# Seven block products instead of eight in the second feed-forward product of a decoder block, its operand sums kept in DRAM

## The chip, the cores and the metric

The kernel runs on one core of one Trainium2 chip. The metric is the time of one execution in microseconds (us), as the median of several runs. A profile comes from one further execution, so its time is given beside its span. The engines are PE (TensorE), DVE (VectorE), ACT (ScalarE), POOL (GpSimd) and SP (SyncE, which here issues all DMAs from one queue, in order); PEld is the loading of PE's stationary operand.

## The reference

A decoder block over 1024 tokens of width 1024, in float32: a state-space branch and a forgetting-attention branch, merged by gates, then cross-attention into 256 memory tokens, then a SwiGLU feed-forward part and a final RMS norm. What matters here is the end:

```python
f_a, f_b = jnp.split(rms_norm(h, norm_ffn[l]) @ w_ffn_in[l], 2, axis=-1)
h = h + (jax.nn.silu(f_a) * f_b) @ w_ffn_out[l]
return rms_norm(h, norm_final)
```

`w_ffn_in` is 1024 x 5632, `w_ffn_out` is 2816 x 1024. So there are 22 tiles of 128 hidden channels, or 11 pairs.

## The kernel before

Every product of float32 operands is made of three matmuls of rounded parts. `split` (L172 to L174) makes the parts: ACT casts a tile to its high part (L173), DVE subtracts that from the tile to get the low part (L174); the matmuls are high x high, high x low and low x high.

**First feed-forward product**, for each hidden tile j of 22 (`start`, `middle`, `end`, L766 and around). It is already done by seven block products in place of eight, each of 12 matmuls of 128 x 128 by 512, which makes 84 per j. The moving operands A11, A12, S4, A22, S1, S2, S3 are sums of quarters of the normed activations. They are built once: `norm_blocks` stores parts to DRAM and `norm_rest` (L714) reads them back (`xr`) and splits them into S4 and A22. The stationary operands are made for every j from two raw weight tiles of 512 KB, `raw` and `rawb`: `w_fetch` loads them (L723), `w_first` splits the first, `w_sums` forms five sums on DVE (L742 to L749) and splits those, `w_last` splits the rest (`wdh`, `wdl`) and so frees the raw tiles. `raw` has two buffers, so the one for j + 2 is loaded when `w_last` of j is done. `end` makes the gated result g of tile j, 128 channels by 1024 tokens: a DVE operation gives the first half of the tokens (L794), and a DVE add (L796), an ACT activation (L797) and a POOL product (L798) the second. g is stored to DRAM as two tiles of 256 KB (`g_d`, L800). The loop runs `start(j)`, `end(j - 1)`, `w_last(j)`, `middle(j)`, `w_first(j + 1)`, `w_sums(j + 1)`, `w_fetch(j + 2)`.

**Second feed-forward product.** For each half hf of the tokens and each j of 22, `o_get` loads 512 KB of `w_ffn_out` (`raw`) and the 256 KB of g (`gr`), splits both (`woh`/`wol`, `gp`), and `o_mm` adds 24 matmuls into eight PSUM banks: four token tiles by two halves of 512 outputs. Loads run three steps ahead in the text. The last four steps of a half are done token tile by token tile. After each tile DVE adds the bank to the residual `hf` (L895, residual read back from `h_d`), ACT sums the squares (L896), `rsqrt` (L188 to L198, one operation of it on POOL, L192) gives the norm's factor, and `scale` (L865) multiplies and stores the result (L867).

**What sets the order.** The text gives an order, but a scheduler of the language fixes the order on each engine when the kernel is built, by its own estimates, and it can move an instruction far from where the text has it. Each engine then runs its list in order and waits where a semaphore says so; SP does the same with the DMAs. Buffers also order the work: `t` has 16 tiles of 128 x 1024 (12 of them hold A11, A12 and S2 during the first product), `big` 16 (S1, S3, S4 and A22), `tmp` four (`rawb`, g), `half` five, `whi` and `wlo` four each, `gbc` and `xs` one each. In the build of before the load of the final norm's gain into `gbc` (L203) stands right behind the last use of the previous gain, in front of the first product's loop.

The functions that the diff touches, with the lines of the profile:

Of the kernel before, what the change touches and what calls it, by code (L numbers as in the profile page):

```python
# [19 lines left out]
P = 128  # L20
D = 1024
L = 1024
NT = 8
# [7 lines left out]
SLOT = 1040  # L31
# [34 lines left out]
def f32(ap):  # L66
    return ap.bitcast(F32)
# [37 lines left out]
class Shared:  # L105
# [5 lines left out]
    def tmp(self, name, dt=F32):  # L111
        return self.pool.tile([P, D], dt, tag="tmp", bufs=4, name=name)
# [356 lines left out]
def stage_tail(B, big, s2, sh, x, glu, aT, gate_d, kv_d, w_fox_o, w_mix_out, g_mq, w_mem_q, w_mem_o, g_ffn,  # L469
               w_ffn_in, w_ffn_out, g_fin, out):  # L470
    nc, V, A, G, T, S, small, ident = B.nc, B.V, B.A, B.G, B.T, B.S, B.small, B.ident
    NS2 = 16

    def bslot(dt=F32, name="b"):
        return big.tile([P, D], dt, tag="big", name=name)

    def slot(dt=F32, name="t"):
        return s2.tile([P, D], dt, tag="t", bufs=NS2, name=name)

    tmp = sh.tmp  # L480
# [99 lines left out]
    sc = float(DH * 2) ** -0.5  # L580
# [84 lines left out]
    g_d = B.dram.tile([NF, 2, P, 512], F32, name="g_d")  # L665
    comb = {}

    def blocks(name, mk):
# [51 lines left out]
    def w_fetch(j):  # L720
        raws[j] = B.wpool.tile([P, SLOT], F32, tag="raw", bufs=2, name="raw")[:, :D], tmp("rawb")
        for r_, c in zip(raws[j], (0, FH)):
            S.dma_start(r_.rearrange("p (k c) -> p k c", k=8),  # L723
                        w_ffn_in[:, c + j * P:c + (j + 1) * P].rearrange("(k p) c -> p k c", p=P))
# [64 lines left out]

    def end(j):  # L790
        b1, b3, a0, a1, c1 = [ev.pop((j, s_)) for s_ in ("b1", "b3", "a0", "a1", "c1")]
        g = tmp("g")
        prod(j, 3, b1, False)
        V.scalar_tensor_tensor(out=g[:, :512], in0=b1, scalar=-1.0, in1=a0, op0=ALU.mult, op1=ALU.mult)  # L794
        prod(j, 4, b3, False)
        V.tensor_add(a1, a1, b3)  # L796
        A.activation(a1, a1, AF.Silu)  # L797
        G.tensor_mul(g[:, 512:], a1, c1)  # L798
        for h in range(2):
            S.dma_start(g_d[j, h], g[:, 512 * h:512 * h + 512])  # L800
# [37 lines left out]
    gfin = B.bcast_gain(s2, g_fin)  # L838
    LAST = 4
    seq = [(hf, j) for hf in range(2) for j in range(NF)]  # L840
    ops, ssq, rs, Hf = {}, {}, {}, {}

    def o_get(n):
        hf, j = seq[n]
        wr = B.wpool.tile([P, SLOT], F32, tag="raw", bufs=2, name="raw")[:, :D]
        S.dma_start(wr, w_ffn_out[j * P:(j + 1) * P, :])
        gr = sh.half("gr")
        S.dma_start(gr, g_d[j, hf])
        w_ = wpair(0) if n < 3 else (bslot(F32R, "woh"), bslot(F32R, "wol"))
        g_ = slot(F32R, "gp")  # L850
        B.split(*w_, wr)
        B.split(g_[:, :512], g_[:, 512:], gr)
        ops[n] = w_, g_

    def o_mm(n, ps, i, c):
        j = seq[n][1]
        (wh, wl), g_ = ops[n]
        cs = slice(512 * c, 512 * c + 512)
        B.mm3(ps, g_[:, i * P:(i + 1) * P], g_[:, 512 + i * P:512 + (i + 1) * P], wh[:, cs], wl[:, cs],
              j == 0, j == NF - 1)  # L860

    def scale(t):
        for c in range(2):
            cs = slice(512 * c, 512 * c + 512)
            V.scalar_tensor_tensor(out=Hf[t][:, cs], in0=Hf[t][:, cs], scalar=rs[t], in1=gfin[:, cs], op0=ALU.mult,  # L865
                                   op1=ALU.mult)
            S.dma_start(out[t * P:(t + 1) * P, cs], Hf[t][:, cs])  # L867

    for n in range(3):
        o_get(n)  # L870
    end(NF - 1)
    for hf in range(2):
        bk = [B.bank(t_) for t_ in ("mm", "mm", "mm", "sc", "sc", "pv", "pv", "misc")]
        for j in range(NF - LAST):
            n = hf * NF + j
            for i in range(4):
                for c in range(2):
                    o_mm(n, bk[2 * i + c], i, c)
            if n + 3 < len(seq):
                o_get(n + 3)  # L880
            if j == NF - LAST - 4:
                for i in range(4):
                    t = 4 * hf + i
                    Hf[t] = slot(name="hf")
                    S.dma_start(Hf[t], h_d[t])
        n0 = hf * NF + NF - LAST
        o_get(n0 + 3)
        for i in range(4):
            t = 4 * hf + i
            ssq[t] = small.tile([P, 2], F32, name="ssq")  # L890
            for c in range(2):
                cs = slice(512 * c, 512 * c + 512)
                for n in range(n0, n0 + LAST):
                    o_mm(n, bk[2 * i + c], i, c)
                V.tensor_add(Hf[t][:, cs], Hf[t][:, cs], bk[2 * i + c])  # L895
                A.activation(B.junk[:, :512], Hf[t][:, cs], AF.Square, scale=1.0 / 32, accum_out=ssq[t][:, c:c + 1])  # L896
            rs[t] = B.rsqrt(ssq[t], parts=2)
            scale(t)
            if hf == 0 and i < 3:
                o_get(NF + i)  # L900


class Glu:
# [349 lines left out]
class Fox:  # L1253
# [350 lines left out]
```

## Time and profile before

| | us |
|---|---|
| median of 3 runs (1645.52 to 1646.85) | 1646.68 |
| the profiled execution | 1651.04 |
| its span on the core | 1649.2 |
| PE busy | 1580.4 |
| DVE busy | 934.6 |
| ACT busy | 639.2 |
| POOL busy | 256.7 |
| granted clock of PE, mean | 0.976 |

The profile gives for each engine the time in which it was busy; for stretches of the span the same by engine, with the granted clock and what the DMAs moved; for groups of like instructions the busy time, the mean of one in ns, the idle time of the engine just before them and what ended it (`<-`); and single instructions in order of time, with start, duration, line, what is written and what is read. A matmul's duration reaches over the start of the next, so a row of busy time does not say how closely they follow each other. `SPq` and `PEq` are the queues of those engines: an `SPq` row is the issue of a DMA, not its transfer.

### The profile page before, as it was taken

The numbers are of one execution on the slowest core, as the hardware profiler recorded it, in microseconds if no ns is written. First come the engines' busy times: TensorE is split into PE (matmuls) and PEld (weight loads), VectorE is DVE, ScalarE is ACT, GpSimd is POOL, SyncE is SP. The second block draws the span as 40 slices with busy tenths as digits, with TensorE's granted clock in tenths as the row PEclk, the third lists the DMA queues.
The fourth block names the chain that finished last, engine by engine and source line by source line (L and its number), as shares of the span: only waits on it lengthen the run. The fifth ranks groups of instructions, "written<-read, shape, count | busy, mean of one in ns | idle before, by whom it ended". The sixth has DMA issues, their size and how long they took to land. (4 is left out here: it accounts for less than half of the span.)

```text
span 1649.2 us, 20384 instructions
## 1 busy us (share of the span) xinstructions
PE 1580.4 (96%) x7445; PEld 1298.6 (79%) x7445; DVE 934.6 (57%) x1761; ACT 639.2 (39%) x1180; POOL 256.7 (16%) x339
## 2 busy tenths in 40 slices
PE   7899599998999999999999989999999999999998
PEld 6688588897677778888888768888888887888886
DVE  6646564424777777773445798555554554535423
ACT  5322233322566654221325665333333333424311
POOL 2007455100111214210002210000010000000000
PEclk7899799999899999999999999999999999999999
DMA  7655557633312544443211254322223224843721
GB/s 250 132 88 99 59 120 125 148 72 40 41 52 60 141 130 130 139 141 117 81 64 52 94 202 144 97 77 78 83 77 96 87 67 143 297 153 134 243 64 51
DMA packets 202339, 184.26 MB, mean 112 GB/s; under 512 B 48232, under 2 KB 156872, under 8 KB 202240
## 3 DMA queue, kind: packets, MB, share of 16 engines
q1 hardware_dynamic: 202240, 182.97, 41.1%
q8 instruction: 58, 0.95, 0.3%
q14 instruction: 41, 0.34, 0.1%
HBM read 136.76 MB, written 44.14 MB: 110 GB/s over the span
## 5 line engine op out<-in xcount | busy, mean ns | idle before, releaser
L174 DVE TENSOR_TENSOR wlo<-raw,whi 128x1024 fp32r<-128x1024 f32 (+2 forms) x129 | 137.1, 1064 | 217.8 <-ACT whi L173 206.1
L173 ACT CAST whi<-raw 128x1024 fp32r<-128x1024 f32 (+2 forms) x132 | 119.2, 906 | 264.5 <-DMA raw<-in_w_in_dram 75.2
L163 PE MATMUL mm<-uh,whi 128*128 128x512 f32 x344 | 140.4, 408 | 0.3 <-DVE mc L1423 0.3
L165 PE MATMUL mm<-uh,wlo 128*128 128x512 f32 x344 | 138.2, 402 | 0.0
L164 PE MATMUL mm<-ul,whi 128*128 128x512 f32 x344 | 137.9, 401 | 0.0
L174 DVE TENSOR_TENSOR wol<-raw,woh 128x1024 fp32r<-128x1024 f32 x41 | 50.2, 1225 | 105.7 <-ACT woh L173 105.4
L798 POOL TENSOR_TENSOR g<-a,c 128x512 f32<-128x512 f32 x22 | 33.8, 1537 | 394.1 <-ACT a L797 394.1
L173 ACT CAST woh<-raw 128x1024 fp32r<-128x1024 f32 x41 | 43.0, 1049 | 112.5 <-PE misc L164 92.8
L192 POOL TENSOR_TENSOR r<-ms,mhalf 128x1 f32<-128x1 f32 x26 | 17.4, 670 | 387.3 <-DVE ms L188 379.1
L165 PEld LDWEIGHTS mm<-uh,wlo 128*128 128x128 f32 x344 | 66.7, 194 | 13.7 <-DVE wlo L174 0.2
L163 PEld LDWEIGHTS mm<-uh,whi 128*128 128x128 f32 x344 | 67.2, 195 | 13.0 <-DVE mc L1423 0.6
L164 PEld LDWEIGHTS mm<-ul,whi 128*128 128x128 f32 x344 | 66.7, 194 | 11.8
L1455 POOL TENSOR_TENSOR pl<-pf,ph 128x512 fp32r<-128x512 f32 (+1 forms) x32 | 36.9, 1152 | 237.9 <-DVE ph L1454 223.3
L1452 ACT ACTIVATE pf<-sc 128x512 f32<-128x512 f32 (+1 forms) x96 | 46.4, 490 | 49.9 <-DVE sc L1448 34.0
L766 PE MATMUL pv<-S3h,we 128*128 128x512 f32 x176 | 58.8, 394 | 2.0 <-ACT S3h L173 2.0
L163 PE MATMUL mm<-woh,gp 128*128 128x512 f32 x123 | 47.8, 389 | 0.0
L164 PE MATMUL mm<-wol,gp 128*128 128x512 f32 x123 | 47.8, 389 | 0.0
L165 PE MATMUL mm<-woh,gp 128*128 128x512 f32 x123 | 47.8, 389 | 0.0
L165 PE MATMUL sc<-uh,wlo 128*128 128x512 f32 x104 | 40.6, 391 | 0.7 <-DVE wlo L174 0.7
L163 PE MATMUL sc<-uh,whi 128*128 128x512 f32 x104 | 40.9, 393 | 0.0
L163 PE MATMUL mm<-yh,whi 128*128 128x512 f32 x104 | 40.7, 392 | 0.0
L766 PEld LDWEIGHTS pv<-S3h,we 128*128 128x128 f32 x176 | 33.3, 189 | 9.4 <-ACT S3h L173 2.4
(574 smaller groups left out, 4577.2 us busy)
## 6 DMA issues: line engine op xcount, KB each, us to landing
raw<-in_w_ffn_out_dram SPq DMA_DIRECT2D x44, 512.0 KB
raw<-in_w_ffn_in_dram SPq DMA_DIRECT2D x22, 512.0 KB
rawb<-in_w_ffn_in_dram SPq DMA_DIRECT2D x22, 512.0 KB
g_d<-g SPq DMA_DIRECT2D x44, 256.0 KB
gr<-g_d SPq DMA_DIRECT2D x44, 256.0 KB
raw<-in_w_in_dram SPq DMA_DIRECT2D x20, 512.0 KB
gate_d<-gs SPq DMA_DIRECT2D x32, 256.0 KB
raw<-in_w_mem_kv_dram SPq DMA_DIRECT2D x8, 512.0 KB
```

What stands on the lines that cost most here:

```text
L163: T.matmul(ps, lh, rh, start=first, stop=False)
L164: T.matmul(ps, lh, rl, start=False, stop=False)
L165: T.matmul(ps, ll, rh, start=False, stop=last)
L173: self.A.copy(hi, src)
L174: (self.G if pool_lo else self.V).tensor_sub(lo, src, f32(hi))
L192: self.G.tensor_tensor(out=r, in0=v, in1=self.mhalf[:, 0:n], op=ALU.pow)
L766: T.matmul(ps, l_[:, k, :], r_, start=first and k == 0 and i == 0, stop=k == 3 and i == 2, skip_group_check=True)
L798: G.tensor_mul(g[:, 512:], a1, c1)
L1452: A.activation(pf[:, off:], ps[:, off:], AF.Exp)
L1455: G.tensor_sub(pl[:, off:], pf[:, off:], f32(ph[:, off:]))
```

## The change

The second product is also done by seven block products. For each pair p of hidden tiles the gated results give four blocks (even or odd tile, first or second half of the tokens) and the weights four (even or odd tile, first or second half of the outputs).

- `end` no longer stores g. For every second j, `gated(p)` forms the four sums of the gated blocks on DVE (each reading two SBUF tiles of 128 x 512, one of them waiting for POOL's product of j) and stores seven left operands to DRAM, `c_d`.
- `out_fetch(p)` loads the two weight tiles of the pair into the buffers `gbc` and `xs`; `out_sums(p)` forms four sums on POOL, in place, and stores each to DRAM, `t_d`. In the text this is one pair per two iterations of the first product's loop. In the build it stands elsewhere: all the loads, the 44 POOL operations and the 44 stores are placed one pair after the other from the point where the gain was loaded before up to the loads of the weights of j = 8, and SP's and POOL's other work stands between them.
- The second product runs product by product (1, 2, 6, 7, 5, 4, 3), each over all 11 pairs: 77 steps. A step loads 256 KB of `c_d` and 256 KB of weights (of `t_d`, or half rows of `w_ffn_out` for products 1, 2 and 3), splits the 128 x 1024 together, and does 12 matmuls into four banks. Two sets of four banks take turns. At the end of a product `o_add` adds or subtracts the set into the residual; a product may go on on top of what its set holds (6 and 5 on 1, 4 on 7, 3 on 5).
- The second half of the tokens is finished after product 4, the first half after product 3, whose last three pairs are done tile by tile, nine matmuls for each.
- The load of the final gain stands after the last `out_sums`.

```diff
     def end(j):
...
-        g = tmp("g")
+        g = gs[j] = tmp("g")
...
         G.tensor_mul(g[:, 512:], a1, c1)
-        for h in range(2):
-            S.dma_start(g_d[j, h], g[:, 512 * h:512 * h + 512])
+        if j % 2:
+            gated(j // 2)
+    def gated(p):
+        ge, go = gs.pop(2 * p), gs.pop(2 * p + 1)
+        a11, a21, a12, a22 = ge[:, :512], ge[:, 512:], go[:, :512], go[:, 512:]
+        s24, s3 = slot(name="s24"), sh.half("s3")
+        for n, a_ in ((1, a11), (2, a12), (4, a22)):
+            S.dma_start(c_d[n, p], a_)
+        V.tensor_sub(s3, a11, a21)
+        V.tensor_sub(a21, a22, a21)
+        V.scalar_tensor_tensor(out=s24[:, :512], in0=a21, scalar=-1.0, in1=a11, op0=ALU.mult, op1=ALU.subtract)
+        V.scalar_tensor_tensor(out=s24[:, 512:], in0=s24[:, :512], scalar=-1.0, in1=a12, op0=ALU.mult,
+                               op1=ALU.subtract)
+        for n, a_ in ((7, s3), (5, a21), (6, s24[:, :512]), (3, s24[:, 512:])):
+            S.dma_start(c_d[n, p], a_)
+    def out_fetch(p):
+        wout[p] = s2.tile([P, D], F32, tag="gbc", bufs=1, name="wo1"), s2.tile([P, D], F32, tag="xs", bufs=1, name="wo2")
+        for i in range(2):
+            S.dma_start(wout[p][i], w_ffn_out[(2 * p + i) * P:(2 * p + i + 1) * P, :])
+    def out_sums(p):
+        w1, w2 = wout.pop(p)
+        b11, b12, b21, b22 = w1[:, :512], w1[:, 512:], w2[:, :512], w2[:, 512:]
+        for n, o, i in ((5, b11, b12), (7, b12, b22), (6, b22, b11), (4, b21, b22)):
+            G.tensor_add(o, o, i)
+            S.dma_start(t_d[n, p], o)
     for j in range(2, NF):
...
+        if j % 2 == 0:
+            out_fetch(j // 2 - 1)
+        else:
+            out_sums(j // 2 - 1)
+            if j == NF - 1:
+                out_fetch(NP - 1)
-    gfin = B.bcast_gain(s2, g_fin)
...
+    seq = [(n, p) for n in ORDER for p in range(NP)]
+    def o_get(m):
+        n, p = seq[m]
+        r_ = slot(name="or")
+        S.dma_start(r_[:, :512], c_d[n, p])
+        if n < 4:
+            j, c = 2 * p + (n > 1), 512 * (n > 2)
+            src = w_ffn_out[j * P:(j + 1) * P, c:c + 512]
+        else:
+            src = t_d[n, p]
+        S.dma_start(r_[:, 512:], src)
+        hl = wpair(0) if m < 4 else (bslot(F32R, "oh"), bslot(F32R, "ol"))
+        B.split(*hl, r_)
+        ops[m] = hl
+    def o_mm(m, i):
+        n, p = seq[m]
+        hi, lo = ops[m]
+        ps = sets[n in (2, 7, 4)][i]
+        gi = slice(i * P, (i + 1) * P)
+        for k, (l_, r_) in enumerate(((hi, hi), (hi, lo), (lo, hi))):
+            T.matmul(ps, l_[:, gi], r_[:, 512:], start=n < 3 and p == 0 and k == 0 or n == 7 and p == 0 and k == 0,
+                     stop=p == NP - 1 and k == 2, skip_group_check=True)
...
+    for m in range(4):
+        o_get(m)
+    end(NF - 1)
+    out_sums(NP - 1)
+    gfin = B.bcast_gain(s2, g_fin)
+    for m, (n, p) in enumerate(seq):
+        if n == 3 and p >= NP - LAST:
+            break
+        for i in range(4):
+            o_mm(m, i)
+        if m + 4 < len(seq):
+            o_get(m + 4)
...
+    for i in range(4):
+        for m in range(len(seq) - LAST, len(seq)):
+            o_mm(m, i)
+        o_add(3, i)
+        square(i, 1)
+        finish(i)
```

More of the change, by code (lines that the diff above doesn't have):

```diff
@@ L835, in stage_tail @@
             w_fetch(j + 2)
-    gfin = B.bcast_gain(s2, g_fin)
[L839 to L862, printed above, removed]
+        if j % 2 == 0:
[4 more added lines that the diff above has]
+                out_fetch(NP - 1)
+    LAST = 3
+    ORDER = (1, 2, 6, 7, 5, 4, 3)
@@ new lines, in stage_tail @@
+    seq = [(n, p) for n in ORDER for p in range(NP)]
+    ops, Hf = {}, {}
+    ssq = small.tile([P, 2 * NT], F32, name="ssq", bufs=1)
+    def o_get(m):
[11 more added lines that the diff above has]
+        ops[m] = hl
@@ new lines, in o_mm, with o_add @@
+    def o_mm(m, i):
[6 more added lines that the diff above has]
+                     stop=p == NP - 1 and k == 2, skip_group_check=True)
+    def o_add(n, i):
+        t, c, op = {1: (0, 0, ALU.add), 2: (0, 0, ALU.add), 6: (4, 0, ALU.add), 7: (4, 1, ALU.subtract),
+                    5: (4, 1, ALU.subtract), 4: (4, 0, ALU.add), 3: (0, 1, ALU.subtract)}[n]
+        h = Hf[t + i][:, 512 * c:512 * c + 512]
+        V.tensor_tensor(out=h, in0=h, in1=sets[n in (2, 7, 4)][i], op=op)
@@ L863, in scale, with square, finish @@
+    def square(t, c):
+        A.activation(B.junk, Hf[t][:, 512 * c:512 * c + 512], AF.Square, scale=1.0 / 32,
+                     accum_out=ssq[:, 2 * t + c:2 * t + c + 1])
+    def finish(t):
+        r = B.rsqrt(ssq[:, 2 * t:2 * t + 2], parts=2)
         for c in range(2):
             cs = slice(512 * c, 512 * c + 512)
-            V.scalar_tensor_tensor(out=Hf[t][:, cs], in0=Hf[t][:, cs], scalar=rs[t], in1=gfin[:, cs], op0=ALU.mult,
+            V.scalar_tensor_tensor(out=Hf[t][:, cs], in0=Hf[t][:, cs], scalar=r, in1=gfin[:, cs], op0=ALU.mult,
@@ L866, in scale @@
                                    op1=ALU.mult)
             S.dma_start(out[t * P:(t + 1) * P, cs], Hf[t][:, cs])
-    for n in range(3):
-        o_get(n)
+    for m in range(4):
+        o_get(m)
     end(NF - 1)
[L872 to L875, printed above, removed]
-            for i in range(4):
[L877 to L900, printed above, removed]
@@ new lines, in stage_tail @@
+    out_sums(NP - 1)
+    gfin = B.bcast_gain(s2, g_fin)
+    sets = [[B.bank(t_) for t_ in tags] for tags in (("sc", "sc", "misc", "mm"), ("mm", "mm", "pv", "pv"))]
+    for m, (n, p) in enumerate(seq):
[5 more added lines that the diff above has]
+            o_get(m + 4)
+        if n < 3 and p in (2, 4, 6, 8):
+            t = 4 * (n - 1) + p // 2 - 1
+            Hf[t] = slot(name="hf")
+            S.dma_start(Hf[t], h_d[t])
+        if p == NP - 1:
+            for i in range(4):
+                o_add(n, i)
+                if n in (2, 5):
+                    square(i if n == 2 else 4 + i, n // 3)
+                if n == 4:
+                    square(4 + i, 0)
+                    finish(4 + i)
```

6 lines of the change are left out of this document (5 added, 1 removed).

## The prediction

> **What bounds the kernel now.** I read the page first, then busy time by stage, then the instructions in order of time at the places that the change touches. Times in us are from the start of the span. In the rows by stage the columns are the stretch, its length, busy time and (instructions) of PE, PEld, DVE, ACT and POOL, granted clock, DMA share, GB/s.
>
> ```profile
> PE 1580.4 (96%) x7445; PEld 1298.6 (79%) x7445; DVE 934.6 (57%) x1761; ACT 639.2 (39%) x1180; POOL 256.7 (16%) x339
> 971.00:1007.87 36.87, 29.26 (x115) 22.42 (x114) 33.17 (x73) 20.44 (x49) 2.46 (x2) 0.86 0.48 157
> 1007.87:1032.56 24.69, 24.69 (x111) 20.44 (x109) 17.63 (x26) 9.99 (x17) 3.06 (x2) 1.00 0.49 149
> 1032.56:1375.28 342.72, 342.72 (x1514) 283.79 (x1513) 184.32 (x271) 126.57 (x199) 28.16 (x18) 1.00 0.26 82
> 1401.17:1641.70 240.53, 239.91 (x1056) 198.04 (x1056) 98.41 (x140) 72.90 (x110) 5.53 (x8) 1.00 0.47 159
> 1641.70:1649.20 7.50, 0.00 (x0) 0.00 (x0) 2.79 (x7) 1.12 (x4) 0.55 (x1) 0.80 0.26 99
> ```
>
> The fourth row is 18 iterations of the first feed-forward product, the fifth the whole second product. In both PE has no idle time at the full clock, DVE is busy for half of the time, ACT and DMA less. The end of the kernel is set by PE from 1007.87 on. The second row is different: DVE has work for 33.17 of 36.87, and PE already loses time there.
>
> What a matmul costs is its spacing, not its duration:
>
> ```profile
> L163 PE MATMUL mm<-woh,gp 128*128 128x512 f32 x123 | 47.8, 389 | 0.0
> 1013.52 0.39 PE L766 MATMUL mm<-A11h,whi 128*128 128x512 f32 x1
> 1032.56 0.39 PE L766 MATMUL mm<-A11h,whi 128*128 128x512 f32 x1
> ```
>
> The duration is 0.389, but the two rows below are the first matmuls of iterations j = 2 and 3, with 84 between: 19.04 / 84 = 0.2267 each (the second product: 240.53 / 1056 = 0.2278, idle moments included). Iteration j of that loop begins at S(j) = 1013.52 + 19.04 (j - 2).
>
> **The change, part by part.**
>
> *1. Matmuls.* Before: 44 steps of 24 = 1056. After: 77 steps (7 products, 11 pairs) of 12 = 924. That is 132 fewer at 0.2267: **-29.9**. Nothing else bounds this stage now, so they count in full if the rest keeps up.
>
> *2. Does the rest keep up in the second product?* A step is now 12 x 0.2267 = 2.72 us and needs one split of 1024 columns on ACT and on DVE, and 512 KB.
>
> ```profile
> L174 DVE TENSOR_TENSOR wol<-raw,woh 128x1024 fp32r<-128x1024 f32 x41 | 50.2, 1225 | 105.7 <-ACT woh L173 105.4
> L173 ACT CAST woh<-raw 128x1024 fp32r<-128x1024 f32 x41 | 43.0, 1049 | 112.5 <-PE misc L164 92.8
> 1420.00:1450.00 30.00, 30.00 (x135) 24.82 (x134) 12.30 (x15) 9.28 (x13) 0.00 (x0) 1.00 0.75 272
> ```
>
> DVE needs 1.23 and ACT 1.05 of 2.72. The 28 additions of a bank to the residual (16 before) use one set of four banks while PE fills the other; in the changed build the splits stand six steps ahead of most of them. The loads are 512 KB / 2.72 = 193 GB/s, 271 in the first ten steps, where 2 MB of residual come too; the last row shows 272 carried with PE never idle. Cost 0, from 0 to the price of the fourth rival.
>
> *3. Where the second product starts.* The first four steps are fetched ahead. In SP's queue the loads of the fifth stand behind the stores of the last pair's sums, which wait for the last gate product on POOL.
>
> ```profile
> 1400.50 0.39 PE L766 MATMUL pv<-A22h,wdl 128*128 128x512 f32 x1
> 1405.18 1.30 POOL L798 TENSOR_TENSOR g<-a,c 128x512 f32<-128x512 f32 x1 [16.05 <-ACT a L797]
> ```
>
> The first row is the last matmul of the first feed-forward product. POOL's product comes 4.7 later, behind DVE splits that the changed order puts elsewhere; with only an add of 0.69 and an activation about as long ahead I take it as done at 1403.7. Three DVE sums of 0.69 end at 1405.8, the loads issue at 1406.5 and land at 1410.6 (3.5, see 6, and the stores ahead of them), the splits end at 1412.9. PE wants them at 1400.7 + 4 x 2.72 = 1411.6, the second half 0.2 later: **+1.0** (0 to 3). Behind the waiting DMAs stand only the next steps' loads.
>
> *4. The end.* Before, a tile's chain after its last matmul takes 7.5:
>
> ```profile
> 1641.73 0.69 DVE L895 TENSOR_TENSOR hf<-hf,misc 128x512 f32<-128x512 f32 x1 [0.43 <-PE misc L165]
> 1643.27 0.21 DVE L188 TENSOR_SCALAR ms<-ssq 128x1 f32<-128x1 f32 x1 [0.85 <-ACT junk L896]
> 1643.56 0.55 POOL L192 TENSOR_TENSOR r<-ms,mhalf 128x1 f32<-128x1 f32 x1 [4.89 <-DVE ms L188]
> 1644.72 1.41 DVE L865 SCALAR_TENSOR_TENSOR hf<-hf,r,gbc 128x512 f32<-128x512 f32 x2
> ```
>
> Tiles now follow each other every 9 matmuls, 2.04, not every 24. The first add comes at E - 6.1 (E: PE's end), its chain on DVE (add, wait for ACT, ms, wait for POOL, three small ones, two scales) takes 5.2, and each later tile adds 2.85 (0.69 + 0.21 + 0.46 + 1.41 and gaps), with a wait for POOL in the last. DVE ends at E + 7.8, where it ended at E + 4.4 (1646.1). **+3.4** (2 to 5).
>
> *5. The sums in the first product's loop, four on DVE per pair.* In iterations with no other new work they cost nothing. DVE is idle for (342.72 - 184.32) / 18 = 8.8 per iteration; they are 4 x 0.69 per pair of iterations, and the wait for POOL's product in the middle is about 2.2. Every second raw weight load is issued 4.5 later for it, and three more 256 KB stores pass. PE waits only if that load is over 6.8 later: ACT's cast of it then stands ahead of the copy a that PE's sixth product needs at S + 10.9. Without this cover it is 4.5 per pair.
>
> *6. The sums of the output weights.* This is the dear part. The text asks for one pair per two iterations; the build does not keep that. On POOL and in SP's queue all 22 loads, 44 adds (128x512, two inputs) and 44 stores stand packed, from where the gain was loaded (first row below) to the weights of j = 8.
>
> ```profile
> 984.21 0.40 SPq L203 DMA_DIRECT2D gbc<-in_norm_final_dram  x1
> 1387.84 1.29 POOL L798 TENSOR_TENSOR g<-a,c 128x512 f32<-128x512 f32 x1 [17.11 <-ACT a L797]
> 1027.73 1.77 POOL L798 TENSOR_TENSOR g<-a,c 128x512 f32<-128x512 f32 x1 [13.33 <-ACT a L797]
> 1028.27 1.78 DVE L174 TENSOR_TENSOR we<-rawb,we 128x512 fp32r<-128x512 f32 x1
> 1216.58 0.68 DVE L174 TENSOR_TENSOR we<-rawb,we 128x512 fp32r<-128x512 f32 x1
> ```
>
> Alone, such a POOL operation takes 1.29. Beside DVE operations with two SBUF inputs they take turns: at 1027.73 POOL takes 1.77, and DVE's split, 0.68 elsewhere, takes 1.78 and ends 0.55 after POOL does. So I charge DVE up to 1.29 for each of the 44 adds while it has such work. The Trainium skill, in "GPSIMD Engine Reference", section "8. Key points", names DVE instructions with two SBUF inputs (and those in a 2-port mode) as the ones that contend with POOL for their shared SBUF interfaces. By that rule the DVE operations that read PSUM pass beside an add; the rows above show only the other kind. If an add held every DVE operation, (a) below would be about 1.5 more and the sum -9.
>
> Where that bites:
>
> ```profile
> 1001.53 0.32 SPq L714 DMA_DIRECT2D xr<-r_d  x1
> 1005.01 0.71 ACT L173 CAST S4h<-xr 128x256 fp32r<-128x256 f32 x2 [0.93 <-DMA xr<-r_d]
> 1005.90 0.75 DVE L174 TENSOR_TENSOR S4l<-xr,S4h 128x256 fp32r<-128x256 f32 x2
> 1006.42 0.45 PE L766 MATMUL mm<-S4l,wdh 128*128 128x512 f32 x1
> 1008.43 0.53 SPq L723 DMA_DIRECT2D rawb<-in_w_ffn_in_dram  x1
> 1013.79 1.16 DVE L742 TENSOR_TENSOR raw<-raw,rawb 128x512 f32<-128x512 f32 x1 [1.43 <-DMA rawb<-in_w_ffn_in_dram]
> 1014.42 0.34 SPq L800 DMA_DIRECT2D g_d<-g  x1
> 1017.59 0.37 SPq L723 DMA_DIRECT2D rawb<-in_w_ffn_in_dram  x1
> 1019.08 1.81 DVE L174 TENSOR_TENSOR wlo<-raw,whi 128x1024 fp32r<-128x1024 f32 x2
> 1024.40 0.39 PE L766 MATMUL mm<-S2h,whi 128*128 128x512 f32 x1
> 1216.73 0.37 SPq L723 DMA_DIRECT2D raw<-in_w_ffn_in_dram  x1
> ```
>
> A 512 KB load lands in 3.5 (1001.53 to 1005.01), a store in about 3 (1014.42 to 1017.59, where the next load waits for it).
>
> (a) To 1013. PE's matmul at 1006.42 waits for DVE's split of the fourth xr at 1005.90. By then pair 0 (adds from 988 to 998) has held DVE for about 4, pair 1 (1002 to 1010) for 3; the fourth xr waits for DVE to free its buffer and comes at 1009, not 1005. I put that split at 1012.4: 6.5 lost.
>
> (b) j = 2. SP reaches rawb not at 1008.43 but after pair 1's four stores and pair 2's first load, at 1016; DVE's first sum (1013.79) comes at 1021.3. Then a sum waits for the gate product of j = 0, which stands behind an add on POOL, and three adds take turns with it: the splits that ended at 1020.9 end at 1034. PE wants them at 1024.40 + 6.5 = 1030.9: 3 more.
>
> (c) j = 3 to 8. A pair's chain is: last store 3, second load 3.5, three adds 3.9, turns with DVE 1.4: 11.8. With SP's waits for gate stores in between I get pair 2 done at 1028, 3 at 1046, 6 at 1081, 9 at 1116. raw for j + 2 is issued at S(j) + 12.8 now (S(10) = 1203.9, 1216.73); PE does not notice up to about S + 24 when the pair closes in that iteration. For j = 6 and 8, with S shifted by 9.5, I get 1085.5 against 1085 and 1125.5 against 1124.5: with DVE's waits, 2.5.
>
> Sum 12. And a PE that waits loses its clock:
>
> ```profile
> 975.00:980.00 5.00, 2.57 (x6) 1.51 (x6) 4.19 (x11) 0.63 (x1) 2.46 (x2) 0.72 0.01 5
> 980.00:985.00 5.00, 4.33 (x17) 3.82 (x18) 3.79 (x8) 1.63 (x5) 0.00 (x0) 0.60 0.94 266
> ```
>
> After the wait before 977 the clock is 0.60 to 0.72 for ten us. For (a) and (b) I add 3: **+15**. Bounds: 4, if PE has more slack than I see; 45, if each pair's chain takes 17.
>
> "TensorE: Matmul & The Clock Gate" of the Trainium skill, section "Part 1: The HAM clock gate (the "warmup" mystery)", puts the drop to half rate after an idle window of about 3.4 us; if every wait stayed shorter, the 3 would be 0 and the sum -13.5.
>
> **Sum.** -29.9 + 1.0 + 3.4 + 15 = -10.5 on the profiled execution, 1651.0 with 1649.2 of it the span: 1640.5. That execution lies 4.4 above the median of the runs, 1646.7; a difference moves over unchanged: **1636.2**.
>
> **Rivals.**
>
> *The cover holds.* PE notices little of the weight sums: 0 to 5. For it: DVE idles for 8.8 per iteration from 1032 on. Against: 33.17 of 36.87 before. 1646.7 - 25.5 + 2 = 1623. Chance 0.18.
>
> *The chain of the weight sums sets the pace: slower.* raw for j = 8 stands behind 10.25 pairs on SP. From 984 it may be issued at S(6) + 24 = 1113.7 without harm, so at a period of T the loss is 10.25 T - 129.7. At 15.1 it eats the 25.5 that is gained. 17 costs 44.6: 1646.7 + 19 = 1666. For it: loads, stores and raw weights together ask for about 250 GB/s there, and every SP wait for a gate store or a raw slot stops the chain. Against: 11.8 from the rows. Chance 0.28, half of it between 1649 and 1660.
>
> *Two turns.* If DVE and POOL took turns as above but SP were never late, only (a) and the DVE part of (b) would stay, about 8: 1629. That is inside the forecast.
>
> *DMA bounds the second product.* It moves 77 x 0.52 + 8.4 = 49 MB in 209 us, 234 GB/s. [...] The 272 above speaks against it. Chance 0.08.
>
> *The matmuls do not go.* The changed build has them 132 fewer; no chance given.
>
> **How the numbers follow.** The forecast has 0.46, its own range 1626 to 1643. A measurement tells 0.2% or 3.3 us from no change. Faster: nearly all of 0.46, and 0.18: 0.61. Same: the upper edge of the forecast and the cheapest slower cases, 0.09. Slower: 0.30. Leaving out a tenth on each side gives 1621 to 1660.
>
> **What would show it.** 924 matmuls spaced by 0.227 in the second product, without idle time beyond the first steps (1, 2); PE idle before the fifth step (3); the last DVE scale 7.8 after the last matmul (4); PE idle behind S4l and behind a DVE split between 990 and 1040, and POOL adds of over 1.29 beside DVE operations of over 1.2 (6a, b); raw loads of j = 6 and 8 issued late on SP behind stores of the sums (6c); from j = 10 on PE without idle time (5). It is wrong if PE loses over 25 before j = 9, or nothing.

## The result, and the profile after

The changed kernel takes 1659.14 us (median of 4 runs, 1656.22 to 1660.78), beside 1646.76 for the kernel before on the same chip: a ratio of 1.0074, 95% interval 1.0057 to 1.0092. So it is slower by 12.4, where 10.5 faster was forecast. The profiled execution took 1660.78, 1659.1 of it the span.

The page's row of engines and busy time by stage, columns as in the prediction's first fence:

```profile
PE 1561.3 (94%) x7313; PEld 1279.1 (77%) x7313; DVE 1007.2 (61%) x1806; ACT 647.1 (39%) x1169; POOL 319.2 (19%) x383
971.00:1007.87 36.87, 25.97 (x90) 19.61 (x89) 33.78 (x64) 17.70 (x42) 7.72 (x6) 0.77 0.61 196
1012.53:1044.20 31.67, 28.15 (x109) 21.78 (x108) 25.85 (x27) 9.89 (x18) 17.37 (x13) 0.89 0.66 216
1044.20:1182.38 138.18, 121.67 (x506) 97.79 (x504) 90.14 (x109) 40.52 (x67) 50.86 (x35) 0.95 0.62 209
1182.38:1410.86 228.48, 228.48 (x1010) 189.19 (x1008) 136.54 (x204) 83.23 (x133) 17.10 (x12) 1.00 0.32 103
1437.03:1648.80 211.77, 209.90 (x918) 172.99 (x916) 116.14 (x138) 87.10 (x103) 4.98 (x7) 0.99 0.63 218
1648.80:1659.07 10.27, 0.00 (x0) 0.00 (x0) 6.18 (x16) 1.06 (x4) 1.09 (x2) 0.72 0.44 168
```

PE has the 132 matmuls fewer, and its stage, the sixth row, is 28.8 shorter than the 240.53 of before. The stretches of the third, fourth and fifth row begin and end with the first matmul of an iteration. Iteration 3 begins at 1044.20, where it began at 1032.56: 11.6 lost. Iterations 3 to 8 (fourth row) take 138.18 where 6 x 19.04 = 114.24 were wanted: 23.9 more. PE is busy for only 121.67 of them, so 16.5 of the 23.9 are waits; the other 7.4 are matmuls at a slower clock (0.95). Iterations 9 to 20 (fifth row) are 12 x 19.04 to the hundredth. The end takes 10.27 where it took 7.50. Together 11.6 + 23.9 - 28.8 + 2.8, and 0.3 around the start of the second product, make 9.8; the spans differ by 9.9. The whole surprise lies before iteration 9, in the weight sums: 35.6 where 15 was forecast.

One of these losses in order of time (start, duration, engine, line; lines of the first product's loop up to the POOL product are one lower than before, so that product is L797 here):

```profile
1082.70 0.63 ACT L796 ACTIVATE a<-a 128x512 f32<-128x512 f32 x1 [0.56 <-DVE a L795]
1083.38 1.27 POOL L833 TENSOR_TENSOR wo<-wo 128x512 f32<-128x512 f32 x1 [5.64 <-DMA wo<-in_w_ffn_out_dram]
1088.71 1.29 POOL L797 TENSOR_TENSOR g<-a,c 128x512 f32<-128x512 f32 x1
1090.04 0.69 DVE L815 TENSOR_TENSOR g<-g 128x512 f32<-128x512 f32 x1 [7.37 <-POOL g L797]
1092.58 0.68 DVE L174 TENSOR_TENSOR wdl<-raw,wdh 128x512 fp32r<-128x512 f32 x1
1093.31 0.38 SPq L722 DMA_DIRECT2D raw<-in_w_ffn_in_dram  x1
1097.11 0.62 ACT L173 CAST wdh<-rawb 128x512 fp32r<-128x512 f32 x1 [8.58 <-DMA c_d<-s]
1099.08 1.04 ACT L173 CAST whi<-raw 128x1024 fp32r<-128x1024 f32 x1 [0.83 <-DMA raw<-in_w_ffn_in_dram]
1101.42 1.67 DVE L741 TENSOR_TENSOR raw<-raw,rawb 128x512 f32<-128x512 f32 x1
1102.61 3.32 POOL L833 TENSOR_TENSOR wo<-wo,wo 128x512 f32<-128x512 f32 x2
1103.01 1.77 DVE L742 TENSOR_TENSOR raw<-raw,rawb 128x512 f32<-128x512 f32 x1
1104.70 0.68 DVE L774 TENSOR_TENSOR a<-a,sc 128x512 f32<-128x512 f32 x1
1106.41 1.75 DVE L174 TENSOR_TENSOR wlo<-raw,whi 128x512 fp32r<-128x512 f32 x1
1112.62 0.57 ACT L782 COPY a<-mm 128x512 f32<-128x512 f32 x1
1113.24 0.80 PE L765 MATMUL mm<-S1h,whi 128*128 128x512 f32 x1 [6.83 <-ACT a L782]
```

Two things meet here. First, a gate product whose input was ready at 1083.3 starts at 1088.7, behind four adds of which the first had waited 5.64 for its load. DVE's gated sum waits 7.37 for it, DVE's split that frees `raw` stands behind that sum, and `raw` is only then loaded. Second, when `raw` has landed, the sums and splits that make the next weights run beside POOL's adds and take 1.67 to 1.77 in place of 0.68. Only the one that reads PSUM (1104.70) does not. PE waits 6.83 for a copy on ACT that stands behind all this. The cast at 1097.11 had waited 8.58 for the store of a gated sum, but it ends before `raw` has landed, 0.83 ahead of the cast at 1099.08, so it does not set this wait.

That is what I saw before any experiment. I took the order of SP's queue for the main cause: loads and stores of the sums packed there, 14.7 per pair (the first pair's first add starts at 988.1, the eleventh's at 1135.4), with the raw weights behind them. The rivals were DVE's turns with POOL, the gate product behind adds, and the DMA traffic itself.

### The profile page after: what moved, and what is told of

Its sections match the earlier page's. It is cut to its first block, busy times and chain, and to the rows that moved or that the text cites. A ratio compares the mean times of both kernels' runs of the same rounds, so it can differ in the third digit from the quotient of the medians.

```text
span 1659.1 us, 20567 instructions
## 1 busy us (share of the span) xinstructions
PE 1561.3 (94%) x7313; PEld 1279.1 (77%) x7313; DVE 1007.2 (61%) x1806; ACT 647.1 (39%) x1169; POOL 319.2 (19%) x383
## 5 line engine op out<-in xcount | busy, mean ns | idle before, releaser
L174 DVE TENSOR_TENSOR ol<-or,oh 128x1024 fp32r<-128x1024 f32 x73 | 88.5, 1223 | 66.2 <-ACT oh L173 66.0
L173 ACT CAST oh<-or 128x1024 fp32r<-128x1024 f32 x73 | 76.7, 1052 | 98.1 <-PE pv L904 34.3
L797 POOL TENSOR_TENSOR g<-a,c 128x512 f32<-128x512 f32 x22 | 31.6, 1438 | 280.2 <-ACT a L796 280.2
L765 PE MATMUL mm<-S1h,whi 128*128 128x512 f32 x88 | 37.3, 424 | 11.7 <-ACT a L782 11.7
L833 POOL TENSOR_TENSOR wo<-wo 128x512 f32<-128x512 f32 x22 | 32.2, 1464 | 77.4 <-DMA wo<-in_w_ffn_out_dram 50.3
L996 POOL TENSOR_TENSOR sg<-sg,ga 128x512 f32<-128x512 f32 x16 | 29.7, 1875 | 72.4 <-DVE sg L989 72.4
L765 PE MATMUL mm<-S2h,whi 128*128 128x512 f32 x88 | 36.4, 414 | 7.1 <-ACT a L772 4.7
L765 PEld LDWEIGHTS pv<-S3h,we 128*128 128x128 f32 x176 | 33.3, 189 | 12.4 <-ACT we L173 3.7
L904 PE MATMUL mm<-oh 128*128 128x512 f32 x106 | 41.5, 391 | 0.0
L904 PE MATMUL mm<-ol,oh 128*128 128x512 f32 x106 | 41.2, 389 | 0.0
```

Source lines behind the costliest of these rows:

```text
L173: self.A.copy(hi, src)
L174: (self.G if pool_lo else self.V).tensor_sub(lo, src, f32(hi))
L765: T.matmul(ps, l_[:, k, :], r_, start=first and k == 0 and i == 0, stop=k == 3 and i == 2, skip_group_check=True)
L833: G.tensor_add(o, o, i)
L904: T.matmul(ps, l_[:, gi], r_[:, 512:], start=n < 3 and p == 0 and k == 0 or n == 7 and p == 0 and k == 0, stop=p == NP - 1 and k == 2, ski ...
L996: self.B.G.tensor_mul(self.out[j][:, cs], self.out[j][:, cs], ga)
```

## The experiments

**1 to 4.** The kernel before ran at 1647.93 beside these.

`no_wsums`: no weight sums.

```diff
-        if j % 2 == 0:
-            out_fetch(j // 2 - 1)
-        else:
-            out_sums(j // 2 - 1)
...
-            src = t_d[n, p]
+        j, c = 2 * p + (n in (2, 3, 4, 6)), 512 * (n in (3, 5, 6))
+        src = w_ffn_out[j * P:(j + 1) * P, c:c + 512]
```

> Leaves out the weight sums altogether (no loads of whole rows into the two buffers, no POOL adds, no stores to t_d); products 4 to 7 read a half row of w_ffn_out in place of their sum, so what is computed in them is not the reference. All else is the changed kernel. Theory (the whole of the unexpected loss is the weight sums, packed between 984 and 1143): the loss of 35.6 up to j = 9 goes, and what is left is what the other terms gave, -25.7 against the kernel before: 1621, between 1618 and 1626. Rival (some other part of the change, the sums of gated blocks or the longer chain at the end, takes part of it): 1635 or more.

Measured 1623.18, ratio 0.9848 (0.9834 to 0.9863). The weight sums cost 36, and all else in the change gains what was forecast.

`spread`: the loads of a pair wait their turn in SP's queue.

```diff
-            out_fetch(j // 2 - 1)
+            with B.tc.issue_after(getattr(held[0], "ins", held[0])):
+                out_fetch(j // 2 - 1)
```

(`held[0]` is the last load of `w_fetch`. The edge binds only the scheduler: on SP's queue the pair's loads come after that load. It adds no wait.)

> The changed kernel with nothing left out; only the loads of a pair of output weights are held behind the raw weight load of j + 2 on SP, so that the build keeps one pair per two iterations of the first product's loop. Theory (the loss comes from the packing: pair after pair in SP's queue, 14.7 per pair, with the raw weight loads behind them): a pair now has 38 and PE does not notice; 1621 to 1627, a few us more than without the sums only at the end of the loop, where the last two pairs stand together. Rival A (each pair costs PE its 3.2 wherever it stands, by DVE and POOL taking turns): 1652 to 1660, as the changed kernel. Rival B (some other part of the change): 1640 or more.

Measured 1648.34, ratio 1.0004 (0.9990 to 1.0018). The packing is gone and 25 of the 36 are still there: my theory failed here. Two neighbouring iterations by stage, the first without a pair, the second with one:

```profile
1093.17:1112.21 19.04, 19.04 (x85) 15.78 (x84) 12.49 (x19) 6.66 (x11) 1.29 (x1) 1.00 0.24 81
1112.21:1135.02 22.81, 20.94 (x85) 16.84 (x84) 13.70 (x16) 7.79 (x12) 8.34 (x5) 0.93 0.59 198
```

The second in order of time:

```profile
1118.70 1.67 DVE L741 TENSOR_TENSOR raw<-raw,rawb 128x512 f32<-128x512 f32 x1
1119.90 3.33 POOL L833 TENSOR_TENSOR wo<-wo,wo 128x512 f32<-128x512 f32 x2
1120.29 1.77 DVE L742 TENSOR_TENSOR raw<-raw,rawb 128x512 f32<-128x512 f32 x1
1122.58 1.19 DVE L743 TENSOR_TENSOR rawb<-rawb 128x512 f32<-128x512 f32 x1
1123.70 1.77 DVE L174 TENSOR_TENSOR wlo<-raw,whi 128x512 fp32r<-128x512 f32 x1
1130.57 0.50 PE L765 MATMUL mm<-S1h,whi 128*128 128x512 f32 x1 [1.87 <-ACT a L782]
```

No gate product is late here, yet one pair costs PE 22.81 - 19.04 = 3.8. On DVE these four operations between the landed weights and their splits take 6.40. In `no_wsums`, without POOL adds, the same four are these:

```profile
1092.24 0.69 DVE L741 TENSOR_TENSOR raw<-raw,rawb 128x512 f32<-128x512 f32 x1
1092.85 0.69 DVE L742 TENSOR_TENSOR raw<-raw,rawb 128x512 f32<-128x512 f32 x1
1093.57 0.69 DVE L743 TENSOR_TENSOR rawb<-rawb 128x512 f32<-128x512 f32 x1
1094.77 0.68 DVE L174 TENSOR_TENSOR wlo<-raw,whi 128x512 fp32r<-128x512 f32 x1
```

So the chain is stretched by some 3.7. PE waits for 1.87 of it and loses as much again to a slow clock behind that wait (0.93 in the second row). DVE is busy for only 13.70 of the 22.81; its idle time is no help, since it is not in this chain.

`short_adds`: packed, POOL's adds cut short.

```diff
-            G.tensor_add(o, o, i)
+            G.tensor_add(o[:, :8], o[:, :8], i[:, :8])
```

> The 44 POOL adds work on 8 of their 512 columns, so that the sums are not those of the reference; all loads, all stores and all waits of the chain stay, packed as in the changed kernel. Theory (the pair's period decides): three adds between the second load and the last store and the turns with DVE go, 3.9 + 1.4 of 14.7, so the period is near 9.4, under the 12.7 (129.7 / 10.25) at which raw for j = 8 comes in time; about a third of the loss before j = 3 stays: 1626, between 1621 and 1636. Rival A (DVE and POOL taking turns is all of it): 1621. Rival B (the DMA traffic of the packed sums, over 200 GB/s, is what delays the raw weights): 1650 to 1660.

Measured 1633.10, ratio 0.9906 (0.9890 to 0.9923). With the same DMA traffic, 26 of the 36 go with the adds' time, so traffic alone is at most 10. The run lies in the range of my theory as well: it cannot tell DVE's turns with POOL from the pace of the pairs, since both shrink with the adds.

`loop_on_act`: raw loads and gate stores on ACT's queue.

```diff
-            S.dma_start(r_.rearrange("p (k c) -> p k c", k=8),
+            A.dma_start(r_.rearrange("p (k c) -> p k c", k=8),
...
-            S.dma_start(c_d[n, p], a_)
+            A.dma_start(c_d[n, p], a_)
```

(The last pair of lines stands for both store loops of `gated`.)

> The changed kernel with nothing left out; the raw weight loads and the stores of the gated blocks are issued on ACT's queue, so that in the loop SP's queue holds only the weight sums, still packed. Theory (the raw weights are late because they stand behind waiting loads and stores of the sums in SP's one queue): most of the loss from j = 3 on, 24, goes; what DVE loses to POOL's adds up to j = 3 stays, 8 to 18, and ACT pays for waits of its own, which the spacing of the iterations from j = 10 on would show: 1630 to 1642. Rival A (turns of DVE and POOL, and gate products behind adds): 1650 to 1660. Rival B (DMA traffic): 1650 to 1660.

Measured 1666.97, ratio 1.0114 (1.0095 to 1.0133): slower still. The longest wait of DVE between 1030 and 1115 (in all, times, longest):

```profile
DVE g L815 <- POOL g L797: 24.7, 2, 18.1
```

and POOL at that time:

```profile
1099.16 1.26 POOL L833 TENSOR_TENSOR wo<-wo 128x512 f32<-128x512 f32 x1 [4.13 <-DMA wo<-in_w_ffn_out_dram]
1104.41 1.26 POOL L797 TENSOR_TENSOR g<-a,c 128x512 f32<-128x512 f32 x1
```

Here the gate product stood behind adds of the next pair, which waited for loads, and DVE waited 18.1 for it. It suggests that POOL's order has a price of its own. On SP's order it is inconclusive, because ACT's queue brought long waits of its own.

**5 to 8.** Before: 1646.28. The theory now: an add on POOL costs what it takes from DVE's chain, wherever that chain is what PE waits for.

`spread_dve`: spread, with the adds on DVE, behind the last split of the raw weights (`held[1]` is that split).

```diff
-            G.tensor_add(o, o, i)
+            V.tensor_add(o, o, i)
...
-            out_sums(j // 2 - 1)
+            with B.tc.issue_after(getattr(held[1], "ins", held[1])):
+                out_sums(j // 2 - 1)
```

> Nothing left out. One pair per two iterations as before, but the four adds stand on DVE, behind the last split of the raw weights (S + 18 of the iteration after the one that loads the pair), where DVE waits for the next raw weights; POOL keeps only the gate product. Theory now (what costs is POOL's add beside DVE's two-SBUF operations: in the spread build the sums of the raw weights, which PE waits for, take 1.67 to 1.77 each in place of 0.68): the cost of 25 that the spread build still has goes to 0 to 6, so 1623 to 1629. Rival (the loads of the pair, which stand with the raw loads, make raw late): 1638 to 1648, as the spread build.

Measured 1622.25, ratio 0.9853 (0.9836 to 0.9869): as without weight sums. The 17 iterations from 4 to 20:

```profile
1051.63:1375.29 323.66, 323.66 (x1429) 268.13 (x1428) 225.87 (x325) 117.47 (x188) 24.09 (x17) 1.00 0.47 161
```

PE is never idle at the full clock, with DVE busy for 70% of the time.

`spread_short`: spread, with the short adds on POOL (both edits above).

> The spread build with POOL adds of 8 of 512 columns, so that the sums are not those of the reference; all its loads, stores and waits stay. Theory now (the adds' time beside DVE): 1623 to 1628. Rival (the pair's loads beside the raw loads): 1638 to 1648.

Measured 1621.21, ratio 0.9845 (0.9829 to 0.9860). The loads and stores of a pair cost nothing once they are spread.

`spread_late`: spread, POOL's full adds held behind the gate product (`held[1]` is that product).

> Nothing left out. The spread build with POOL's four adds held behind the gate product of the iteration after the load, so that they stand from S + 14 to S + 21 beside the last splits and not beside the sums of the raw weights. Theory now: what an add costs depends on what DVE does beside it; here two or three splits and the freeing of raw are late by 1 each, then the start of the next weights: about half of 25, 1630 to 1640. Rival A (every add costs PE the same wherever it stands, 0.57): 1646 to 1650. Rival B (the pair's loads): 1646 to 1650.

Measured 1629.07, ratio 0.9892 (0.9876 to 0.9908). The same 44 adds on the same engine cost 19 less than in `spread`, because of what stands beside them. Rivals A and B are out. The iterations 4 to 20, and the only long PE wait behind them:

```profile
1046.93:1370.62 323.69, 323.69 (x1430) 268.07 (x1429) 206.60 (x291) 116.44 (x188) 76.00 (x52) 1.00 0.47 161
1414.03 0.79 PE L906 MATMUL sc<-oh 128*128 128x512 f32 x1 [7.79 <-ACT oh L173]
```

In these iterations the full adds on POOL cost PE nothing at all. Nearly all of the 7 that separate this run from `spread_dve` is one wait, 7.79 where `spread_dve` has 1.9, for the fifth step of the second product: the last gate product stands on POOL behind the last pair's adds (it starts at 1402.26), and the fifth step's loads stand on SP behind the stores that wait for it.

`sums_alone`: the kernel before with `out_fetch` and `out_sums` added.

> The kernel before, with the weight sums alone added: loads, POOL adds and stores, in the same place of the text, and packed by the build in the same way; the sums are stored and not used, so the output stays that of the reference. It has no sums of gated blocks, so DVE never waits for POOL's gate product in the first product's loop. Theory (turns of DVE and POOL and late raw weights, no part for the gated sums): the weight sums cost the 36 that they cost in the changed kernel, 1646.7 + 36 = 1683, from 1678 to 1688. Rival (half of the cost needs DVE to wait for a gate product that stands behind adds on POOL): 1660 to 1670.

Measured 1682.20, ratio 1.0217 (1.0200 to 1.0234): +35.9, the same 36. So the gated sums are not needed for the price; a part of a few us could hide in the intervals.

**9 to 12.** Before: 1647.37 for the first three, 1646.73 for the fourth.

`best`: `spread_dve` with four pairs done tile by tile at the end and six steps fetched ahead.

```diff
-    LAST = 3
+    LAST = 4
...
-    for m in range(4):
+    for m in range(6):
         o_get(m)
...
-        if m + 4 < len(seq):
-            o_get(m + 4)
+        if m + 6 < len(seq):
+            o_get(m + 6)
```

> Nothing left out. The spread build with the adds on DVE (measured at 1622.3), with six steps of the second product fetched ahead of the last gated sums in place of four, and the last four pairs done tile by tile in place of three. The wait of 1.9 before the fifth step goes (and the slow clock behind it, some 0.5), and tiles follow each other every 2.72 in place of 2.04, against 2.8 of DVE's chain for each, so the last tile queues for DVE by 0.2 in place of 2.1: 1622.3 - 2.4 - 1.9 = 1618.0, between 1616 and 1621. If the end or the start is set by something else: 1622 to 1625.

Measured 1619.81, ratio 0.9834 (0.9813 to 0.9854). It beats both kernels, but its interval overlaps that of `spread_dve`. The wait before the fifth step is gone. The end, from the last matmul on, is not shorter:

```profile
1607.21:1617.46 10.25, 0.00 (x0) 0.00 (x0) 5.62 (x15) 0.91 (x4) 1.10 (x2) 0.67 0.40 153
```

DVE in it:

```profile
1609.08 0.16 DVE L196 TENSOR_TENSOR rt<-r 128x1 f32<-128x1 f32 x1 [0.66 <-POOL r L192]
1609.15 0.68 DVE L914 TENSOR_TENSOR hf<-hf,mm 128x512 f32<-128x512 f32 x1
1609.75 0.15 DVE L197 SCALAR_TENSOR_TENSOR rt<-rt,ms 128x1 f32<-128x1 f32 x1
```

The scales of the four tiles start on DVE at 1602.08, 1606.87, 1610.13 and 1612.92, so they follow each other by 4.8, 3.3 and 2.8 and not by 2.72. The build puts a tile's add into the middle of another tile's small operations, and DVE waits for POOL besides. The chain on DVE still ends last.

`gate_on_dve` (the changed kernel with the gate product on DVE) and `short_gate_dve` (the same with short adds):

```diff
-        G.tensor_mul(g[:, 512:], a1, c1)
+        V.tensor_mul(g[:, 512:], a1, c1)
```

> The changed kernel, nothing left out, packed as it is, with full adds on POOL and the gate product on DVE. If the two costs add up (turns of DVE with the adds about 25, the gate product behind adds about 10): 1659 - 10 = 1649, between 1646 and 1653. If the gate product behind adds is most of the 36: 1630 or less. If it is nothing: 1657 to 1661.

Measured 1654.68, ratio 1.0050 (1.0028 to 1.0071): 4.5 less than the changed kernel, though the two intervals overlap.

> The changed kernel, packed as it is, with POOL adds of 8 of 512 columns (so the sums are not those of the reference) and the gate product on DVE instead of POOL. With the short adds alone it was 1633.1, against 1621.2 for short adds that are spread. Theory (what the packing itself costs is that the gate product stands on POOL behind adds that wait for their loads, and DVE's sums and splits wait for it): the 10 of it that are lost from j = 5 on go, 1622 to 1626, with all iterations from j = 5 on at 19.04. Rival (raw weights late behind the waiting loads and stores on SP): 1631 to 1634. An iteration that is longer than 19.04 from j = 10 on would be the price of the gate product on DVE.

Measured 1629.86, ratio 0.9892 (0.9870 to 0.9914): 3.2 less than short adds alone, and two iterations from 5 on still take 20.89 and 23.89. So the gate product behind adds is worth some 3 to 5, not 10; both runs point the same way, but here too the intervals overlap (0.9890 to 0.9923 with short adds alone), so the size is rough. In this run the longest waits on ACT are these:

```profile
ACT wdh L173 <- DMA c_d<-s: 22.0, 4, 8.8
```

The tile `wdh` takes the buffer of a gated sum `s24` and waits until its store, late on SP, has landed.

`short_gate_act`: as that, with these stores on ACT's queue (`S` to `A` in the last line of `gated`).

> As the run with short adds and the gate product on DVE (1629.9; the sums are not those of the reference), and besides the four stores of gated sums that DVE makes are issued on ACT's queue, so that they no longer stand behind waiting loads and stores of the weight sums on SP. In that run the cast of wdh waited 7.7 and 8.8 on ACT for the store of s24, whose slot it takes, with the copy of c that PE waits for behind it. Theory (what is left of the packing's cost from j = 5 on, 6.7, is this store): 1622 to 1625. Rival (raw weights that are late themselves): 1628 to 1631. Iterations over 19.04 from j = 10 on would be the price of the stores on ACT.

Measured 1633.35, ratio 0.9916 (0.9888 to 0.9944): no gain. In `loop_on_act` the move to ACT's queue had brought waits of its own, and here the iterations 3 and 5 take 23.08 and 25.56, so it stays open whether the store is a part of what is left.

**13 and 14.** Before: 1647.76.

`short_loop_act`: `short_gate_dve` with the edit of `loop_on_act`.

> As the packed run with short adds and the gate product on DVE (1629.9; the sums are not those of the reference), with the raw weight loads and the stores of the gated blocks on ACT's queue, so that in the first product's loop SP's queue holds the weight sums alone. Theory (what packing costs without the adds' time, about 9, is that raw loads and gate stores stand behind waiting loads and stores of the sums on SP): 1622 to 1626, of which 2 would be the price of ACT's queue (iterations at 19.1 to 19.2 from j = 10 on). Rival (the transfers share the DMA engines, and raw lands late whatever queue issues it): 1630 to 1636.

Measured 1643.20, ratio 0.9968 (0.9951 to 0.9986). Worse again, so neither side is shown.

`dve_adds`: one letter.

```diff
-            G.tensor_add(o, o, i)
+            V.tensor_add(o, o, i)
```

> The changed kernel, nothing left out and packed by the build in the same way, with the 44 full adds on DVE in place of POOL; they stand between the sums of the raw weights on DVE, which waits for each pair's loads. Theory (turns of POOL and DVE are 25 of the 36, the packing about 10): about 1633, plus what DVE loses when it waits for a pair's load in its own order, which no run has shown yet: 1633 to 1650. If the adds cost PE the same on either engine: 1656 to 1662.

Measured 1628.47, ratio 0.9877 (0.9855 to 0.9899). This is the plainest run of all: the sums are still packed, and 30.7 of the 36 are gone. All adds, by count, min/median/max in ns, and first to last start, in the changed kernel and here:

```profile
L833 POOL TENSOR_TENSOR wo<-wo x22: 1263/1404/2068, 988.1 to 1141.0; 128x512 f32<-128x512 f32 x22
L833 POOL TENSOR_TENSOR wo<-wo,wo x22: 1279/1467/1628, 991.5 to 1139.3; 128x512 f32<-128x512 f32 x22
```

```profile
L833 DVE TENSOR_TENSOR wo<-wo x22: 679/692/1666, 991.2 to 1153.3; 128x512 f32<-128x512 f32 x22
L833 DVE TENSOR_TENSOR wo<-wo,wo x22: 678/683/691, 1003.0 to 1152.6; 128x512 f32<-128x512 f32 x22
```

The chain of the pairs is even longer here, 15.3 per pair (the eleventh begins at 1144.7), and PE loses about 6 to it, not 36. Most of that is one iteration, j = 7, which takes 26.56 (1106.24 to 1132.80). The pace of the pairs was not the price. The page's rows of `dve_adds` and, for comparison, of `no_wsums`:

```profile
PE 1548.7 (95%) x7313; PEld 1269.9 (78%) x7313; DVE 1004.7 (62%) x1850; ACT 647.3 (40%) x1169; POOL 257.9 (16%) x339
```

```profile
PE 1545.3 (95%) x7313; PEld 1270.0 (78%) x7313; DVE 977.4 (60%) x1806; ACT 647.9 (40%) x1169; POOL 252.4 (16%) x339
```

The 44 adds on DVE make DVE busy for 27.3 more. The 44 adds on POOL made it busy for 1007.2 - 977.4 = 29.8 more with the same 1806 instructions, so by turns alone. Moving them to POOL saved DVE nothing.

**What the 36 are made of.** The adds' time on POOL is about 26 (1659.1 to 1633.1 with short adds, packed; 1648.3 to 1621.2, 27, spread). The gate product behind adds is roughly 3 to 5. From 5 to 9 stay when the adds are packed but POOL holds up nothing (`dve_adds` and `short_gate_dve` against 1621 to 1623), and go when they are spread. Whether that rest is SP's order or the shared transfers stays open: none of the three kernels that took something off SP's queue was faster, and on ACT's queue new waits came up.

## Why the prediction was wrong, point by point

PE lost 35.6 before j = 9, over the 25 that the prediction named as a sign that it is wrong.

- *Step 1 (matmuls) and step 3 (start of the second product):* right. -29.9 + 1.0 = -28.9 was forecast for the stage, -28.8 measured. PE's wait before the fifth step was 1.9, not 1.0, with a slow clock behind it; but the 240.53 of before held 1.1 of idle moments that went as well.
- *Step 2 (the rest keeps up):* right. PE has no other wait in the stage, at 218 GB/s. So the fourth rival, that DMA bounds this stage, did not happen; no run shows a price for it.
- *Step 4 (the end):* right in kind; 2.8 where 3.4 was forecast. The last scale on DVE ends 7.2 after the last matmul, not 7.8.
- *Step 5 (gated sums cost nothing):* right. Iterations 9 to 20 take 19.04 with them. But the reason given, 8.8 idle on DVE per iteration, was read too widely, see 6c.
- *Step 6a and 6b:* right in size: 6.5 + 3, and 3 for the clock, against 11.6 at the start of iteration 3. 6b is right in its mechanism too: DVE's first sum comes at 1022.85 where 1021.3 was forecast, and the splits end at 1034.1 where 1034 was. In 6a the wait was not the one named, so part of the agreement is luck. PE waited only 0.7 for S4l, since the build had put other matmuls first; it waited 3.3 up to 998.61 for ACT's cast of `we`, behind DVE operations that stood beside the first pair's adds, and from 1000 to 1005 its clock was 0.52.
- *Step 6c (j = 3 to 8): this is the step that failed, 2.5 forecast and 23.9 measured.* It asked only when SP issues the raw load and whether PE notices, and it put DVE's turns with POOL into the pace of the pair (1.4 of 11.8). It never charged them to the chain from the landed raw weights over DVE's sums and splits to the copy on ACT that PE waits for, although step 6b had charged such turns for j = 2. `spread`, where the chains are no longer packed and only this charge is left, still costs 25. The other part of 6c, that `raw` is issued late, did happen, and by more than forecast: `raw` for j = 6 goes out at 1093.31, 26.0 after iteration 4 began at 1067.28, in place of 12.8. By the prediction's own cover of 24 that would be worth some 2 of the 6.83 that PE then waits.
- *Two figures in 6c:* by the prediction's formula 1203.9 is the start of j = 12, not of j = 10; the 12.8 drawn from it holds. S(6) + 24 + 9.5 is 1123.2, not 1124.5, which makes the forecast of 6c about 1 too low and does not touch the step that failed.
- *Rivals:* the outcome lies in the range of "the chain of the weight sums sets the pace", but not by its mechanism. Its formula gives 10.25 x 14.7 - 129.7 = 21 for the changed kernel, which lost 35.6, and 10.25 x 15.3 - 129.7 = 27 for `dve_adds`, which lost about 6. "Two turns" had the right mechanism but expected a gain: it counted turns only up to j = 2. Matmuls and DMA went as forecast.
- The sentence from the Trainium skill in 6, "GPSIMD Engine Reference", section "8. Key points" (DVE operations with two SBUF inputs contend with POOL), agrees with the traces shown: mostly 1.67 to 1.77 for those, 0.68 for L774, which reads PSUM, beside the same adds. The sum drawn from it stopped too early.

## What to carry to other kernels

Idle time of an engine is no cover for work that stretches a chain in which each step waits for the last: count the delay along the chain that the bottleneck waits for, not the engine's share of busy time. An elementwise operation moved to POOL beside two-input DVE operations relieved DVE of nothing here; put it on DVE at a place where DVE waits anyway. In `spread_late` the adds on POOL cost the loop nothing either, once they stood where no operation that PE waits for ran beside them; but then the last of them delayed what stood behind them on POOL. When a scheduler packs side work at one spot, tie it to the loop with an ordering edge, and look at what stands beside it as well as at how it is spaced: both were needed to go from 1659 to 1622.

## What the runs showed of the hardware that was not expected

POOL and DVE alternate, one operation each, at 1.7 per round: by itself the add takes 1.29 and the DVE operation 0.68. "SBUF — State Buffer" of the Trainium skill, section "Summary: rules for kernel authors", says that the one that comes second blocks fully until the first is done. Full blocking of both would make a round of 1.29 + 0.68 = 1.97; the 1.7 here is a little less.

PE's clock can fall after shorter waits than the forecast allowed. Four stretches of `spread`, columns as before: a stretch that is a wait but for 0.16, and the 12 matmuls behind it, twice.

```profile
1128.54:1130.57 2.03, 0.16 (x2) 0.00 (x1) 2.03 (x4) 1.10 (x2) 0.45 (x1) 1.00 0.37 132
1130.57:1135.02 4.45, 4.45 (x12) 3.51 (x13) 0.04 (x2) 1.05 (x1) 1.14 (x1) 0.62 0.41 118
1170.38:1173.10 2.72, 0.16 (x1) 0.00 (x0) 2.72 (x5) 1.23 (x3) 0.45 (x1) 1.00 0.52 176
1173.10:1175.82 2.72, 2.72 (x12) 2.27 (x13) 0.02 (x1) 0.00 (x0) 1.16 (x1) 1.00 0.66 192
```

After a wait of 1.87 the granted clock is 0.62 and 12 matmuls take 4.45 in place of 2.72; after one of 2.56 they take 2.72 at 1.00. "TensorE: Matmul & The Clock Gate" of the Trainium skill, section "Part 1: The HAM clock gate (the "warmup" mystery)", names an idle window of about 3.4 us that runs freely. By that rule a wait of 1.87 would not drop the clock; the trace shows that it can, and that a longer one need not. Here the wait of 1.87 cost 3.60 in all, nearly twice its length.
